# Reading the experts' weights in 8 KB pieces per partition, with the channels of their inputs reordered to match

## The chip, the core and the metric

The kernel runs on one core of a Trainium2 chip. A core has TensorE (PE in the profile; its weight loads are PEld), VectorE (DVE), ScalarE (ACT), GpSimd (POOL) and SyncE (SP), on-chip memory of 128 partitions (SBUF), accumulators for TensorE (PSUM) and 16 DMA engines between the chip's main memory (HBM) and SBUF. The metric is the device time of one execution, in microseconds (us). All data are float32. TensorE's fast format here is fp32r, so the kernel splits every operand into a rounded part and a remainder (hi and lo) and forms each product from three matmuls: hi x hi, lo x hi, hi x lo.

## The reference

Two layers of an encoder, 1024 tokens of 1024 channels. Each layer has a token-mixing half (attention and a convolution) and a routed feed-forward half, to which this change belongs:

```python
def expert_choice_ffn(h, w_router, w_gate, w_up, w_down):
    B, S, D = h.shape
    cap = CAPACITY_FACTOR * S // N_EXPERTS                 # 128 tokens
    logits = jnp.einsum('bsd,de->bse', h, w_router).astype(jnp.float32)
    aff = jax.nn.softmax(logits, axis=-1)
    gate, idx = lax.top_k(aff.transpose(0, 2, 1), cap)
    xe = jax.vmap(lambda hb, ib: hb[ib])(h, idx)
    hid = jax.nn.silu(jnp.einsum('becd,edf->becf', xe, w_gate)) * jnp.einsum('becd,edf->becf', xe, w_up)
    ye = jnp.einsum('becf,efd->becd', hid, w_down) * gate[..., None].astype(h.dtype)
    return jax.vmap(lambda ib, yb: jnp.zeros((S, D), yb.dtype).at[ib.reshape(-1)].add(yb.reshape(-1, D)))(idx, ye)
```

Each of the 16 experts takes its 128 best tokens (gather), computes silu(x Wg) * (x Wu), multiplies by Wd, scales, and adds the rows back to their tokens (scatter). Wg, Wu and Wd are 1024 x 1024 for each expert: 4 MB each in HBM, 12 MB an expert.

## The kernel before, in words

A layer runs in stages: token mixing, then the output projection tile by tile (8 tiles of 128 tokens, the loop `for t in range(TT)`), then the router's sort, then the 16 experts. The order of all instructions is written out by hand, and every engine runs its own in that order: an instruction that waits holds back all behind it on its engine.

**Output projection.** For each tile `mix_mm` multiplies, `mix_x` (L956, L957, DVE) adds the result to the residual in `xm`, `mix_norm` (L962, ACT, then two small POOL operations of `rstd`) makes the norm's factor, and `mix_h` makes the experts' input h2: L969 (DVE) scales `xm` by row and column, L970 adds a row vector, on POOL for tiles 5, 6 and 7 and on DVE for the others. `h2_store` writes the tile to HBM. The router's logits are computed from `xm`, not from h2, in `affine` (L1115 to L1119), and sorted on DVE.

**Experts.** The three matrices of all experts form a list of 192 chunks of 1 MB for each layer (`chunks`, four to a matrix). `load_w` (L1004, SP's queue) reads chunk i of a matrix, rows 256i to 256i+255, as two blocks of 128 rows: partition p gets row 256i + p and row 256i + 128 + p, two pieces of 4 KB that are no neighbours in HBM. A chunk lands in one of five raw buffers in `F`. `split_w` makes the rounded part on ACT (L118) and the remainder on DVE (L119) into one of seven working sets (`WS`, in the tiles R, flexX and flexC), and then issues the load of the chunk that gets the freed raw buffer. `product` multiplies 128 tokens by one matrix: for each of 4 chunks, 4 x 3 matmuls of 512 columns (L113 to L115), then the splits of later chunks, as far as `ahead()` allows: seven chunks at the layer's start, one less after every 8 chunks multiplied, and two from then on.

The order in one expert e is: product with Wu (up), `hid(...)`, `slots_1h` (L1285, 8 small DVE operations that prepare a later expert's gather), product of the next expert with its Wg (gate), in whose course `hid_t(e)` runs, `silu(...)`, product with Wd (down), `down_out` (L1358), which scales and scatters. `gather` (L1302, POOL's queue) fetches the next expert's 128 rows of h2, and `gather_t`/`trans` (L1314) transposes them on TensorE, so that channel 128k + p of a token lies in partition p of block k; this is the order in which the weight rows lie too.

`silu` (L1342, ACT) reads the gate product from PSUM and writes `sg`, two tiles of 512 hidden channels; `hid` (L1346, DVE) multiplies the up product from PSUM into `sg`; `hid_t` transposes `sg` (L504) and splits it.

```python
        hid(product(xT[e], {2: lambda: gather_t(e + 1, (0,)), 3: lambda: next_x(e + 1)}))
        s3 = e + 3 if e + 3 < NE else None
        if s3:
            slots_1h(s3)
        silu(product(xT[e + 1], {1: (lambda: slots(s3)) if s3 else (lambda: None), 2: lambda: hid_t(e)}))
        if e < NE - 2:
            down_out(e, product(hT2[e]))
```

Of the kernel before, what the change touches and what calls it, by code (L numbers as in the profile page):

```python
# [15 lines left out]
AF = mybir.ActivationFunctionType  # L16
ALU = mybir.AluOpType
AX = mybir.AxisListType
ADD, SUB, MUL = ALU.add, ALU.subtract, ALU.mult

T, D, KT, TT = 1024, 1024, 8, 8
# [4 lines left out]
NE, CAP = 16, 128  # L26
# [16 lines left out]
def trunk(ctx: ExitStack, tc: tile.TileContext, x, c, positions, norm1_g, w_ada, b_ada, w_in, q_latent_g, w_uq,  # L43
# [4 lines left out]
    v, a, g, pe, sp = nc.vector, nc.scalar, nc.gpsimd, nc.tensor, nc.sync  # L48
# [38 lines left out]
    def fw(o, *s):  # L87
        return _view(F, o, s)
# [12 lines left out]
    def ps_s():  # L101
        return psum.tile([128, 1024], F32, name="S")
# [32 lines left out]
    def rstd(dst, ss, n, cols=1):  # L135
        g.tensor_scalar(dst, ss, 1.0 / n, EPS, op0=MUL, op1=ADD)
        g.tensor_tensor(dst, dst, neghalf if cols == 1 else neghalf.to_broadcast([128, cols]), op=ALU.pow)
# [137 lines left out]
    TAPS = [[1, 0, 2, 0, 2, 2, 2, 1], [1, 1, 2, 1, 1, 1, 0, 1], [3, 6, 5], [4, 4], [0, 0, 7, 9, 7, 5, 5, 8], [5, 6], [5, 6], [0, 0, 8, 8, 6, 4, 6, 5], [[], 0, 1], [0], 1, 1, 0]  # L275

    def layer(l):
# [494 lines left out]
        for j, n in ((1, 0), (1, 1), (2, 0), (2, 1)):  # L772
            ps = ps_s()
# [88 lines left out]
        for u in range(U):  # L862
            hd, i = divmod(u, TT)
# [66 lines left out]
        g1, tg, a2, b2, g2 = (fw(o, 1024) for o in (0, 1024, 2048, 3072, VB + 1024))  # L930
        xt = lambda t: fw((8960, 4096)[t % 2] if t else 5120, 1024)
        xm = lambda t: fw((9984, 5120)[t % 2], 1024)
        h2 = lambda t: fw({TT - 2: 1024, TT - 1: 11008}.get(t, (8960, 4096)[t % 2]), 1024)
# [10 lines left out]
        MX, RS = {}, {}  # L944
# [14 lines left out]
        def mix_norm(t):  # L959
# [2 lines left out]
            a.activation(h2(t), xm(t), AF.Square, accum_out=ss)  # L962
            rstd(ss, ss, D)

        def h2_store(t):
            sp.dma_start(h2_d[l][128 * t:128 * t + 128], h2(t))

        def mix_h(t):
            v.scalar_tensor_tensor(h2(t), xm(t), RS[t], a2, op0=MUL, op1=MUL)  # L969
            (g if t == TT - 1 or t in TAPS[6] else v).tensor_tensor(h2(t), h2(t), b2, op=ADD)  # L970
            if t != TT - 2:
                h2_store(t)

# [9 lines left out]
        raw_of = lambda c: fw(11008 if c == 1 else RING[(c - 2) % 5 if c else 0], 4, 512)  # L983

        after = lambda c: 2 if c == 0 else None if c == 1 else c + 5

        WP = [w_gate[l, 0], w_up[l, 0]]
        for e in range(NE - 2):
            WP += [w_gate[l, e + 1], w_down[l, e], w_up[l, e + 1]]
        WP += [w_gate[l, NE - 1], w_up[l, NE - 1], w_down[l, NE - 2], w_down[l, NE - 1]]  # L990
        chunks = [(w, i) for w in WP for i in range(4)]
        NCH = len(chunks)


# [1 line left out]

        def load_w(c):
            if c is not None and c < NCH:
                w, i = chunks[c]
                w = w.rearrange("(k p) f -> p k f", p=128)  # L1000
                raw = raw_of(c).rearrange("p (k n) f -> p k (n f)", n=2)
                for ks in parts(c):
                    r = slice(ks.start // 2, ks.stop // 2)
                    sp.dma_start(raw[:, r], w[:, 2 * i + r.start:2 * i + r.stop])  # L1004

        sctr = [0]

        def split_w(sub=None):
            c = sctr[0]
            if c < NCH:  # L1010
                for ks in parts(c):
                    split(WS[c % NW][0][:, ks], WS[c % NW][1][:, ks], raw_of(c)[:, ks], sub)
                load_w(after(c))
                sctr[0] += 1
# [6 lines left out]
        def split_lo(c, q):  # L1021

            if q % 2 == 0:
                SP_[0] = ps_s()
            ps = SP_[0][:, 512 * (q % 2):512 * (q % 2) + 512]
            pe.matmul(ps, ident, raw_of(c)[:, q], start=True, stop=False)  # L1026
            pe.matmul(ps, neg, WS[c % NW][0][:, q], start=False, stop=True)  # L1027
            if q % 2:
                a.activation(WS[c % NW][1][:, q - 1:q + 1], SP_[0].rearrange("p (q c) -> p q c", q=2), AF.Copy)
            if q == 3:  # L1030
                load_w(after(c))
                sctr[0] += 1
# [88 lines left out]
        for t in range(TT):  # L1121
# [35 lines left out]
            if t == 0:  # L1157
                load_w(0)
                load_w(1)
                pc = ps_m()  # L1160
                for k in range(KT):
                    pe.matmul(pc[:, :NE], AB[l][:, 3, k:k + 1].to_broadcast([128, 128]), wr[:, k], start=(k == 0),
                              stop=(k == KT - 1))
                v.tensor_copy(cr, pc[:, :NE])
                v.scalar_tensor_tensor(a2, a2, 1.0, tg, op0=ADD, op1=MUL)
            else:
                mix_t(t - 1)
# [17 lines left out]
            if t == TT - 1:  # L1185
                load_w(3)
                h2_store(TT - 2)
                split_hi(2)
                if not TAPS[9][0]:
                    split_hi(3)  # L1190
# [11 lines left out]
            if t < TT - 1:  # L1202
                mix_h(t)
# [5 lines left out]
        logits(TT - 1, range(4), 4, 3)  # L1209
        split_lo(2, 2)  # L1210
        mix_h(TT - 1)
        affine(TT - 1)
        load_w(5)
# [108 lines left out]
        def product(lhs, hooks={}, upto=NCH):  # L1322
            ps = ps_s()
            for i in range(4):
                c = pctr[0]
                hl = WS[c % NW]
                for j in range(4):
                    kk, n = 2 * i + j // 2, j % 2
                    mm3(ps[:, 512 * n:512 * n + 512], lhs[0][:, kk], lhs[1][:, kk], hl[0][:, j], hl[1][:, j],
                        kk == 0, kk == KT - 1)  # L1330
                pctr[0] += 1
                while sctr[0] < min(upto, c + 1 + ahead()) and sctr[0] <= c + NW:
                    split_w()
                if i in hooks:
                    hooks[i]()
            return ps

        sg = fw(14688, 512), fw(16832, 512)

        def silu(ps):  # L1340
            for n in range(2):
                a.activation(sg[n], ps[:, 512 * n:512 * n + 512], AF.Silu)  # L1342

        def hid(ps):
            for n in range(2):
                v.tensor_tensor(sg[n], ps[:, 512 * n:512 * n + 512], sg[n], op=MUL)  # L1346

        def hid_t(e):
            hT2[e] = [rw(2048 * (e < NE - 1) + 1024 * i, KT, 128) for i in range(2)]
            for b in range(2):  # L1350
                p = to_heads(lambda k: sg[b][:, 128 * k:128 * k + 128])
                split(hT2[e][0][:, 4 * b:4 * b + 4], hT2[e][1][:, 4 * b:4 * b + 4], p.rearrange("p (k q) -> p k q", k=4))
# [22 lines left out]
        def second():  # L1375
            slots(1)
            gather(1)
            slots_1h(2)

        silu(product(xT[0], {0: second, 2: lambda: slots(2)}))  # L1380

        def next_x(e):
# [4 lines left out]
        for e in range(NE - 1):  # L1387
# [7 lines that stand above are left out]
        hid(product(xT[NE - 1]))  # L1395
        ps = product(hT2[NE - 2], {TAPS[11]: lambda: hid_t(NE - 1)})
        down_out(NE - 1, product(hT2[NE - 1], {TAPS[12]: lambda: down_out(NE - 2, ps)}))


    for l in range(L):  # L1400
        layer(l)
# [25 lines left out]
```

## Time and profile before

| | |
|---|---|
| median of 3 runs | 2317.97 us (2317.94 to 2320.8) |
| the profiled execution | 2317.1 us, span from first to last instruction 2315.3 us |
| PE busy | 2216.0 us (96%) |
| DVE busy | 1906.7 us (82%) |
| ACT busy | 1357.0 us (59%) |
| POOL busy | 430.0 us (19%) |
| bytes moved by DMA | 550.97 MB, mean 238 GB/s |
| loads of expert chunks | 128 + 128 + 126 of 1 MB, and 4 of 0.5 MB |
| granted TensorE clock, mean | 0.988 |

Busy time is the time in which an engine has an instruction running; waits in between are listed with what released them. The span of two layers shows the stages twice: from about 592 to 1160 us, and again from about 1730 to 2303 us, the experts run, and DMA and DVE are busiest; before that lie token mixing and the projection. The chain that ended last is followed back from the last instruction, at each step to what released it. An instruction in it delays the end by what it grows; one outside it does so only after its slack is used up.

### The profile page before, as it was taken

What the parts mean: (1) busy time and instruction counts of PE and PEld (TensorE: products, weight loads), DVE (VectorE), ACT (ScalarE), POOL (GpSimd) and SP (SyncE); (2) the same over time, 40 slices, a digit from 0 to 9 for tenths busy, and PEclk for the clock granted to TensorE, in tenths of its full rate; (3) what the DMA queues carried; (4) which work ended last, traced back from release to release, by engine and by line L of the source; (5) the groups of instructions that cost most, each with busy time, mean ns of one, the idle gap of its engine ahead of it and who ended that gap; (6) DMA issues with size and microseconds to landing.
All of it is one profiled execution on the core that took longest, in us unless ns stands there. A gap on an engine that the chain in (4) does not pass through costs nothing. (4 is left out here: it accounts for less than half of the span.)

```text
span 2315.3 us, 31226 instructions
## 1 busy us (share of the span) xinstructions
PE 2216.0 (96%) x11845; PEld 1798.5 (78%) x11845; DVE 1906.7 (82%) x2648; ACT 1357.0 (59%) x1770; POOL 430.0 (19%) x405
## 2 busy tenths in 40 slices
PE   6999999999999999999969999999999999999997
PEld 3678899886688787788847789888867878787786
DVE  3886888668889999998959868875688899999997
ACT  4324766623666677676741356665247667777675
POOL 1001212201021332322010021121011123231320
PEclk9999999999999999999979999999999999999999
DMA  8472000435899999999956300014369999999996
GB/s 276 160 250 90 18 4 19 142 124 199 291 334 352 378 381 380 372 387 376 356 143 213 135 12 16 1 45 161 124 228 331 340 363 382 379 369 390 377 379 239
DMA packets 179354, 550.97 MB, mean 238 GB/s; under 512 B 12820, under 2 KB 34470, under 8 KB 179204
## 3 DMA queue, kind: packets, MB, share of 16 engines
q1 hardware_dynamic: 169712, 515.35, 59.9%
q0 software_dynamic: 9216, 33.56, 5.6%
q8 instruction: 93, 1.52, 0.3%
q14 instruction: 57, 0.47, 0.1%
q10 hardware_dynamic: 276, 0.07, 0.0%
HBM read 515.35 MB, written 33.59 MB: 237 GB/s over the span
## 5 line engine op out<-in xcount | busy, mean ns | idle before, releaser
L119 DVE TENSOR_TENSOR R<-F,R 128x2048 fp32r<-128x2048 f32 (+1 forms) x294 | 636.5, 2185 | 74.7 <-ACT R L118 74.3
L118 ACT ACTIVATE R<-F 128x2048 fp32r<-128x2048 f32 (+1 forms) x294 | 533.3, 1832 | 66.0 <-DMA F<-in_w_up_dram 23.8
L115 PE MATMUL S<-R,flexX 128*128 128x512 f32 x1096 | 431.8, 394 | 10.0 <-DVE R L119 10.0
L113 PE MATMUL S<-R,flexX 128*128 128x512 f32 x1096 | 439.0, 401 | 0.0
L114 PE MATMUL S<-R,flexX 128*128 128x512 f32 x1096 | 427.6, 390 | 0.0
L304 DVE SCALAR_TENSOR_TENSOR F<-F,cw 128x1024 f32<-128x1024 f32 x240 | 307.6, 1282 | 5.3
L119 DVE TENSOR_TENSOR flexC<-F,flexC 128x2048 fp32r<-128x2048 f32 (+3 forms) x126 | 258.3, 2055 | 16.5 <-ACT flexC L118 16.4
L115 PEld LDWEIGHTS S<-R,flexX 128*128 128x128 f32 x1096 | 205.7, 188 | 64.1 <-DVE R L119 17.0
L118 ACT ACTIVATE flexC<-F 128x2048 fp32r<-128x2048 f32 (+3 forms) x126 | 216.9, 1728 | 49.6 <-DMA F<-in_w_in_dram 14.3
L114 PEld LDWEIGHTS S<-R,flexX 128*128 128x128 f32 x1096 | 206.1, 188 | 42.8 <-DVE flexX L119 0.3
L113 PEld LDWEIGHTS S<-R,flexX 128*128 128x128 f32 x1096 | 206.1, 188 | 39.7 <-ACT flexX L118 0.5
L118 ACT ACTIVATE flexX<-T 128x512 fp32r<-128x512 f32 x128 | 73.1, 597 | 238.3 <-PE T L1314 135.2
L115 PE MATMUL S<-R 128*128 128x512 f32 x480 | 189.5, 395 | 0.0
L113 PE MATMUL S<-flexC,flexX 128*128 128x512 f32 x440 | 176.3, 401 | 0.0
L115 PE MATMUL S<-flexC,flexX 128*128 128x512 f32 x440 | 173.3, 394 | 2.5 <-DVE flexC L119 2.5
L114 PE MATMUL S<-flexC,flexX 128*128 128x512 f32 x440 | 171.9, 391 | 2.4 <-DVE flexX L119 2.4
L1359 POOL DMA_INDIRECT x<-F,idx x16 | 99.9, 6245 | 389.9 <-DVE F L1358 364.5
L1359 POOL DMA_INDIRECT out_dram<-F,idx x16 | 99.1, 6193 | 390.1 <-DVE F L1358 364.7
L578 PE MATMUL m<-F 128*128 128x128 f32 x1024 | 125.2, 275 | 0.3
L578 PEld LDWEIGHTS m<-F 128*128 128x128 f32 x1024 | 119.4, 192 | 1.2 <-DVE R L510 1.2
L113 PE MATMUL S<-R 128*128 128x512 f32 x288 | 118.3, 411 | 0.0
L114 PE MATMUL S<-R 128*128 128x512 f32 x288 | 112.6, 391 | 0.0
(294 smaller groups left out, 4017.5 us busy)
## 6 DMA issues: line engine op xcount, KB each, us to landing
F<-in_w_gate_dram SPq DMA_DIRECT2D x128, 1024.0 KB
F<-in_w_up_dram SPq DMA_DIRECT2D x128, 1024.0 KB
F<-in_w_down_dram SPq DMA_DIRECT2D x126, 1024.0 KB
F<-in_w_ada_dram SPq DMA_DIRECT2D x42, 1024.0 KB
F<-in_x_dram SPq DMA_DIRECT2D x16, 512.0 KB
F<-in_w_in_dram SPq DMA_DIRECT2D x16, 512.0 KB
F<-in_w_out_dram SPq DMA_DIRECT2D x16, 512.0 KB
h<-F SPq DMA_DIRECT2D x16, 512.0 KB
```

The source lines that it names most:

```text
L113: pe.matmul(ps, lh, rh, start=first, stop=False)
L114: pe.matmul(ps, ll, rh, start=False, stop=False)
L115: pe.matmul(ps, lh, rl, start=False, stop=last)
L118: a.activation(hi, src, AF.Copy)
L119: (sub or v.tensor_sub)(lo, src, f32(hi))
L304: taps.append(lambda i=i: v.scalar_tensor_tensor(ACC[j], Y[j][:, i:i + T], w[:, i:i + 1], ACC[j], op0=MUL, op1=ADD))
L578: pe.matmul(po[:, :DV], PTS[u % 2][:, k], V[:, k], start=(k == 0), stop=(k == KT - 1))
L1359: g.indirect_dma_start(out=xm_d, out_offset=bass.IndirectOffsetOnAxis(ap=idx[:, e:e + 1], axis=0), in_=y, in_offset=None, compute_op=ADD)
```

## The change

Weight rows are dealt to the partitions differently. Of Wg and Wu, partition p holds rows 8p to 8p + 7, which are neighbours in HBM (32 KB), and a chunk reads two of these rows: one piece of 8 KB for each partition, 32 KB from the next partition's. Of Wd, partition p holds rows 4p to 4p + 3 of each half, and a chunk reads two of them: pieces of 8 KB, 16 KB apart. The bytes, the number of loads, the buffers and the order stay.

So block k of the experts' input must hold channels 8p + k, and block k of a half of the hidden values channels 4p + k of that half. The gather and the transposes stay as they are; the values are put in that order where they are written: L969, L970 (`mix_h`), L1342 (`silu`) and L1346 (`hid`) now write consecutive elements 128 elements (512 bytes) apart in SBUF, and L970 and L1346 read the operand that was written so with the same step. The same instructions run on every engine in the same sequence; only the access patterns of these four and of the loads differ.

```diff
+        by_row = lambda ap: ap.rearrange("q (p k) -> q p k", k=KT)
...
         def mix_h(t):
-            v.scalar_tensor_tensor(h2(t), xm(t), RS[t], a2, op0=MUL, op1=MUL)
-            (g if t == TT - 1 or t in TAPS[6] else v).tensor_tensor(h2(t), h2(t), b2, op=ADD)
+            hp = h2(t).rearrange("q (k p) -> q p k", k=KT)
+            v.scalar_tensor_tensor(hp, by_row(xm(t)), RS[t], by_row(a2), op0=MUL, op1=MUL)
+            (g if t == TT - 1 or t in TAPS[6] else v).tensor_tensor(hp, hp, by_row(b2), op=ADD)
...
-        WP = [w_gate[l, 0], w_up[l, 0]]
+        gate_w, up_w = ([w[l, e].rearrange("(p k) f -> p (k f)", k=8) for e in range(NE)] for w in (w_gate, w_up))
+        down_w = [w_down[l, e].rearrange("(n p k) f -> p n (k f)", n=2, k=4) for e in range(NE)]
+        WP = [gate_w[0], up_w[0]]
...
-        chunks = [(w, i) for w in WP for i in range(4)]
+        chunks = [w[:, i // 2, 2048 * (i % 2):2048 * (i % 2) + 2048] if len(w.shape) == 3 else w[:, 2048 * i:2048 * i + 2048]
+                  for w in WP for i in range(4)]
...
         def load_w(c):
             if c is not None and c < NCH:
-                w, i = chunks[c]
-                w = w.rearrange("(k p) f -> p k f", p=128)
-                raw = raw_of(c).rearrange("p (k n) f -> p k (n f)", n=2)
+                raw = raw_of(c).rearrange("p q f -> p (q f)")
                 for ks in parts(c):
-                    r = slice(ks.start // 2, ks.stop // 2)
-                    sp.dma_start(raw[:, r], w[:, 2 * i + r.start:2 * i + r.stop])
+                    r = slice(512 * ks.start, 512 * ks.stop)
+                    sp.dma_start(raw[:, r], chunks[c][:, r])
...
+        half = lambda ps, n: ps[:, 512 * n:512 * n + 512].rearrange("q (p k) -> q p k", k=4)
+        sgp = [s.rearrange("q (k p) -> q p k", k=4) for s in sg]
+
         def silu(ps):
             for n in range(2):
-                a.activation(sg[n], ps[:, 512 * n:512 * n + 512], AF.Silu)
+                a.activation(sgp[n], half(ps, n), AF.Silu)
 
         def hid(ps):
             for n in range(2):
-                v.tensor_tensor(sg[n], ps[:, 512 * n:512 * n + 512], sg[n], op=MUL)
+                v.tensor_tensor(sgp[n], half(ps, n), sgp[n], op=MUL)
```

## Rows read from the trace of the kernel before

**Rows 1.** Busy us by stretch; columns: window and length, PE, PEld, DVE, ACT, POOL (instructions), PEclk, DMA share, GB/s:

```profile
900.00:950.00 50.00, 48.77 (x239) 39.23 (x238) 45.51 (x53) 33.76 (x24) 14.61 (x4) 1.00 1.02 370
```

**Rows 2.** Chain that ended last: by engine, and one expert of it (start, us, what):

```profile
PE 20%; DVE 4%; ACT 1%; issue 1%; DMA 0%; POOLq 0%; DVEq 0%
...
2038.37 0.45 PE T L1314 x4
...
2039.33 1.92 ACT R L118
...
2044.16 0.36 DVE F L1346
2044.68 0.68 DVE F L1346
2045.36 1.30 DVE F L1285 x8
2046.66 2.21 DVE flexC L119
2048.92 0.50 PE S L115
```

**Rows 3.** Timeline of PE, first layer's experts (start, us, engine, what, [idle before <- releaser]):

```profile
662.40 0.66 PE L504 MATMUL T<-ident,F 128*128 128x128 f32 x4 [0.39 <-DVE idx L1293]
...
730.84 0.50 PE L115 MATMUL S<-R,flexX 128*128 128x512 f32 x1 [0.62 <-DVE R L119]
...
1055.35 0.50 PE L115 MATMUL S<-R,flexX 128*128 128x512 f32 x1 [0.62 <-DVE R L119]
```

**Rows 4.** Timeline of DVE and PE, the same place in the third expert:

```profile
692.54 2.29 DVE L119 TENSOR_TENSOR R<-F,R 128x2048 fp32r<-128x2048 f32 x1
...
694.90 0.40 PE L115 MATMUL S<-R,flexX 128*128 128x512 f32 x1
```

**Rows 5.** Groups of DVE by line and shape (count | busy us, mean ns of one | idle before):

```profile
L1346 DVE TENSOR_TENSOR F<-S,F 128x512 f32<-128x512 f32 x64 | 41.0, 683 | 0.0
...
L262 DVE TENSOR_TENSOR ab<-T,cols 128x4 f32<-128x4 f32 x16 | 2.6, 160 | 17.9 <-PE T L259 17.9
...
L1267 DVE TENSOR_TENSOR F<-F 128x128 bf16<-128x128 f32 x2 | 1.1, 528 | 0.1
...
L1236 DVE CAST F<-tok_b 128x128 bf16<-128x128 f32 x2 | 0.7, 332 | 0.0
...
L1271 DVE TENSOR_TENSOR F<-T,F 128x120 f32<-128x120 f32 x2 | 0.5, 273 | 0.0
...
L1271 DVE TENSOR_TENSOR F<-T,F 128x8 f32<-128x8 f32 x2 | 0.3, 172 | 0.0
```

**Rows 6.** Timeline of POOL and DVE at the projection's last two tiles, first layer:

```profile
564.48 2.35 POOL L970 TENSOR_TENSOR F<-F 128x1024 f32<-128x1024 f32 x1 [1.51 <-PE m L1109]
...
552.66 2.44 DVE L957 TENSOR_TENSOR F<-F 128x512 f32<-128x512 f32 x1
...
563.08 1.26 DVE L969 SCALAR_TENSOR_TENSOR F<-F,ss 128x1024 f32<-128x1024 f32 x1
...
565.42 1.84 DVE L1119 TENSOR_SCALAR F<-F,st 128x16 f32<-128x16 f32 x1
```

**Rows 7.** Timeline around one `silu`: ACT, DVE, PE:

```profile
917.43 1.09 ACT L1342 ACTIVATE F<-S 128x512 f32<-128x512 f32 x2 [0.32 <-PE S L115]
...
920.35 2.29 DVE L119 TENSOR_TENSOR flexC<-F,flexC 128x2048 fp32r<-128x2048 f32 x1 [0.92 <-ACT flexC L118]
...
923.18 0.39 PE L115 MATMUL S<-flexC,flexX 128*128 128x512 f32 x1
```

**Rows 8.** DMA: rates in 40 slices of 150 to 200 us; 900 to 1100 us; longest DMA wait, first layer's experts:

```profile
GB/s 403 411 396 283 2 29 238 408 408 398 216 174 403 403 393 283 34 202 401 411 400 257 10 180 392 411 410 288 0 149 383 391 177 0 0 0 0 0 0 7
...
DMA packets 19659, 75.53 MB, mean 378 GB/s; under 512 B 1245, under 2 KB 1245, under 8 KB 19648
...
ACT R L118 <- DMA F<-in_w_up_dram: 13.6, 19, 1.5
```

More of the change, by code (lines that the diff above doesn't have):

```diff
@@ L985, in layer @@
         after = lambda c: 2 if c == 0 else None if c == 1 else c + 5
-        WP = [w_gate[l, 0], w_up[l, 0]]
+        gate_w, up_w = ([w[l, e].rearrange("(p k) f -> p (k f)", k=8) for e in range(NE)] for w in (w_gate, w_up))
+        down_w = [w_down[l, e].rearrange("(n p k) f -> p n (k f)", n=2, k=4) for e in range(NE)]
+        WP = [gate_w[0], up_w[0]]
         for e in range(NE - 2):
-            WP += [w_gate[l, e + 1], w_down[l, e], w_up[l, e + 1]]
-        WP += [w_gate[l, NE - 1], w_up[l, NE - 1], w_down[l, NE - 2], w_down[l, NE - 1]]
-        chunks = [(w, i) for w in WP for i in range(4)]
+            WP += [gate_w[e + 1], down_w[e], up_w[e + 1]]
+        WP += [gate_w[NE - 1], up_w[NE - 1], down_w[NE - 2], down_w[NE - 1]]
+        chunks = [w[:, i // 2, 2048 * (i % 2):2048 * (i % 2) + 2048] if len(w.shape) == 3 else w[:, 2048 * i:2048 * i + 2048]
+                  for w in WP for i in range(4)]
         NCH = len(chunks)
```

## The prediction

> **What bounds the kernel now.** I read the windows first, then the chain that ended last, then the timelines of the waits it shows. In the experts' stage TensorE is busy for 48.8 of 50 us at full clock, DVE for 45.5, and the DMA share is 1.02 [rows 1]: three resources look full, and the share of busy time doesn't say which sets the pace. The chain does [rows 2]. It holds PE, DVE and ACT, and DMA rounds to 0%; the loads that this change speeds or slows aren't on it. One expert of it reads: transposes on PE (L1314), a split on ACT and DVE, then on DVE without a gap the two multiplications of `hid` (L1346), `slots_1h` (L1285), the next split (L119), and at its end the PE matmul that needs this split's remainder. So `hid` lies on the path, since the split queued behind it on DVE is what PE waits for.
>
> The stall is small, 0.62 us of idle PE, but it returns in each expert: ten times from 730.84 to 1055.35 us, 36.06 us apart [rows 3], and ten times again in the second layer. The second expert has a smaller one, also behind `hid` (0.39 us, at 662.40) [rows 3]. The third has none, but its split ends at 692.54 + 2.29 = 694.83 and PE uses it at 694.90 [rows 4]: a margin of 0.07 us. The first expert has more lead, and the last ones have no `slots_1h` in the way. That makes 12 experts a layer, 24 in all, in which any lengthening of `hid` goes straight into the time.
>
> **The loads.** 384 chunks of 1 MB come as before, in pieces of 8 KB in place of 4 KB. The rate in full stretches is 400 to 411 GB/s where w_ada is read in 2 KB pieces, and 378 on the average of 900 to 1100 us, with the gathers and scatters in it [rows 8]; pieces were not what held it down there. A faster load lands earlier, ACT's waits for DMA shrink (13.6 us in the first layer's experts for the largest group [rows 8]), and nothing on the chain moves, since the split before `hid` waits for PE's transposes and not for a load [rows 2]. I take 0 for the loads; what covers a slower one is the slack of the third rival below.
>
> **The price of a stride.** No row shows a float32 write with a step of 512 bytes. Consecutive elements cost VectorE (683 - 273) / (512 - 120) = 1.05 ns each, with 148 ns fixed [rows 5] (L1346, and the 120-element form of L1271, which is nearly contiguous). The nearest rows with a step:
> - L1271 on 8 elements 64 bytes apart, a tensor_tensor with one operand in PSUM, the other and the result strided, as in `hid`: 172 ns. Four contiguous elements from PSUM took 160 (L262), four more would be 4.2; the other 7.8 ns over 8 elements are 1.0 ns an element, one more cycle.
> - L1236, 128 elements written 10 bytes apart: 332 against 148 + 134 = 282 ns, 0.4 ns an element. This is the low end.
> - L1267, 128 elements read and written 10 bytes apart: 528 against 282, 1.9 ns an element. This is the high end.
>
> All three are dearer than contiguous. I take 1.0 ns, by L1271, the row nearest in form.
>
> [...]
>
> **The sum.**
> - `hid`: 2 x 512 elements x 1.0 ns = 1.0 us an expert, 24 experts on the path: **+24.0 us** (0.41 x 24 = 9.8 at the low end, 1.95 x 24 = 46.8 at the high one).
> - `mix_h`, L969: 1024 elements, +1.0 us (0.4 to 1.95). Tiles 0 to 5 have cover: PE multiplies throughout and DVE isn't what it waits for. At the last two tiles there is none: L969 of the last tile ends at 564.34, and the softmax of the last tile's logits queues right behind it on DVE, ahead of the sort [rows 6]. Two tiles in two layers: +4.0 us (1.6 to 7.8).
> - `mix_h`, L970 on POOL: it takes 2.35 us, and DVE's L957 and L1119, behind the last two tiles' adds, took 2.44 and 1.84 us and ended about when POOL did [rows 6], L1119 for 16 elements. DVE is held there until POOL is through, so what the add grows, the chain to the sort grows. No row shows POOL with a step. It is bounded by 0 and by a doubling, 2.35 us; I take the 1.0 us of DVE's row, lying between. Two adds in two layers: +4.0 us (0 to 9.4). For tile 5 the matmuls behind it cover the add.
> - `silu`, on ACT: 1.09 us for two, 0 to 2 us more. The split behind it is through at 920.35 + 2.29 = 922.64 on DVE, PE takes it at 923.18 [rows 7]: a margin of 0.54 us. ACT has no strided row at all; I take half of DVE's, 0.5 us, which the margin covers: 0. If it grows by 1.0, 0.46 x 24 = 11 us come on top.
> - `h2_store`, gather, transposes, matmuls, and the SP queue: the same instructions in the same places, 0.
>
> Together +32 us on the profiled execution's 2317.1 us: 2349.1. The median of the runs is 0.9 above that execution, which gives **2350 us**. The low ends together give +11.4, 2329; the high ends +64, 2383, and with a `silu` of that price (1.41 x 24 = 34) 2416.
>
> **The rivals.**
> 1. The strides cost nothing, or the loads' pieces change nothing either: 2318 us. For it: L1271's excess is 8 ns on a short instruction, where fixed costs are uncertain, and the two larger rows write 2-byte elements. Against it: three rows of three are dearer. Chance 0.23.
> 2. Faster. DMA sets the pace after all: a chunk's late landing delays ACT's split, DVE's behind it, and by the whole expert the split that PE waits for. With earlier landings the 10 stalls of 0.62 us in each layer go: 12.4 us, 2305 us. For it: the DMA share is 1.02 and ACT waited for loads [rows 1, 8]. Against it: the stalls are equal to hundredths over ten experts and both layers, and the split before `hid` waits for PE [rows 2, 3]. It decides only if the strides cost less than the 0.6 us of a stall. Chance 0.10.
> 3. The loads get slower: the 128 pieces of a load, neighbours before, now lie 32 or 16 KB apart. With `hid` grown an expert takes 37.1 us, for which 378 x 36.06 / 37.06 = 368 GB/s are needed; below that, loads set the pace, and at 340 GB/s an expert takes 40.1 us: about 24 x 4 = 97 us over the time before, 2415. The pieces of w_ada, 24 KB apart, reached 400 GB/s and more [rows 8], which speaks against it. Chance 0.04. [...]
>
> **How the numbers follow.** The forecast with its bounds, 2329 to 2383, has 0.59, the joint high end above 2385 about 0.04. A run of this kernel tells about 0.2%, 4.6 us, from no change. Slower by more takes the forecast, its high end and rival 3: 0.67. Same takes rival 1: 0.23. Faster takes rival 2: 0.10. For 8 in 10 the range goes from 2313, which takes in rival 1, to 2385; it leaves out most of rival 2, rival 3 and the joint high end, less than 0.2. The likeliest case's own range is 2329 to 2383.
>
> **What will show it.** Right: the row of `hid` (683 ns) grows to about 1.2 us and L969 (1.26) to 2.3; PE's stall behind `hid` grows from 0.62 to about 1.6 us in each expert, and experts stand 37.1 us apart; L1119 of the last tile and POOL's add grow together; ACT's waits for DMA shrink or stay, without effect. Wrong: `hid` stays at 683 ns (rival 1 or 2), the stall goes (rival 2), PE or ACT waits for loads at lengths of microseconds (rival 3), or `hid` grows and the experts' distance doesn't, which would mean that DVE had slack that I don't see.

## The result, and the profile after

The change is slower: 2368.68 us in the median of 4 runs (2364.89 to 2376.73), against 2319.12 (2317.94 to 2320.8) for the kernel before on the same chip. The ratio is 1.0218, 95% interval 1.0206 to 1.0230. That is +49.6 us where the forecast had +32: inside the range of 2313 to 2385, the direction right, the sum too small. The profiled execution took 2364.89 us, its span is 2363.1, that is 47.8 more than the span before.

In the changed file the lines have moved: `mix_h` is L973 and L974 (L969, L970 before), `silu` L1351 (L1342), `hid` L1355 (L1346), the softmax's last step L1125 (L1119), `slots_1h` L1291, `trans` L1320. First the groups of instructions by line and shape (count | busy us, mean ns of one | idle before) of the changed kernel, for the four that write with a step; behind them the same of the kernel before for `mix_h` on DVE and `silu`:

```profile
L1355 DVE TENSOR_TENSOR F<-S,F 128x512 f32<-128x512 f32 x64 | 67.4, 1100 | 0.0
L1351 ACT ACTIVATE F<-S 128x512 f32<-128x512 f32 x64 | 66.6, 1151 | 12.9 <-PE S L115 12.9
L973 DVE SCALAR_TENSOR_TENSOR F<-F,ss 128x1024 f32<-128x1024 f32 x16 | 32.7, 2044 | 15.7 <-POOL ss L137 15.6
...
L974 DVE TENSOR_TENSOR F<-F 128x1024 f32<-128x1024 f32 x10 | 19.8, 1983 | 0.3
L974 POOL TENSOR_TENSOR F<-F 128x1024 f32<-128x1024 f32 x6 | 17.5, 2918 | 13.2 <-PE m L1115 8.9 <-DVE F L973 4.4
```

```profile
L1342 ACT ACTIVATE F<-S 128x512 f32<-128x512 f32 x64 | 34.8, 596 | 12.7 <-PE S L115 12.7
L969 DVE SCALAR_TENSOR_TENSOR F<-F,ss 128x1024 f32<-128x1024 f32 x16 | 20.5, 1280 | 15.7 <-POOL ss L137 15.4
L970 DVE TENSOR_TENSOR F<-F 128x1024 f32<-128x1024 f32 x10 | 12.2, 1225 | 0.3
```

All four grew. `hid` stood at 683 ns [rows 5]: 417 ns more for 512 elements, 0.81 ns each. L973 was 1280 ns, so 0.75 ns an element more; L974 on DVE was 1225 (+0.74), on POOL 2364 (+0.54). `silu` was 596: 555 ns more, 1.08 ns an element, the dearest of all, and it is on ACT, for which there had been no row.

Next the timeline of PE in the first layer's experts (start, us, engine, what, [idle before <- releaser]), to be held against the same places in [rows 3, 4]:

```profile
667.29 0.66 PE L504 MATMUL T<-ident,F 128*128 128x128 f32 x4 [1.17 <-DVE idx L1299]
...
703.06 0.66 PE L504 MATMUL T<-ident,F 128*128 128x128 f32 x4 [0.36 <-DVE idx L1299]
...
774.53 0.50 PE L115 MATMUL S<-R,flexX 128*128 128x512 f32 x1 [1.45 <-DVE R L119]
786.95 0.51 PE L115 MATMUL S<-R,flexX 128*128 128x512 f32 x1 [0.26 <-DVE R L119]
811.91 0.50 PE L115 MATMUL S<-R,flexX 128*128 128x512 f32 x1 [1.45 <-DVE R L119]
```

The stall behind `hid` is 1.45 us where it was 0.62, the second expert's 1.17 where it was 0.39, and the third expert, which had a margin of 0.07, now has one of 0.36. Behind `hid` of the fourteenth and fifteenth expert there was none before; now there are 0.47 and 0.44 us. Behind twelve of a layer's `silu`s there is a second stall, of 0.22 to 0.28 us, that wasn't there before. Around `silu` the timeline shows why:

```profile
894.55 2.10 ACT L1351 ACTIVATE F<-S 128x512 f32<-128x512 f32 x2 [0.31 <-PE S L115]
...
896.43 1.94 ACT L118 ACTIVATE R<-F 128x2048 fp32r<-128x2048 f32 x1
...
898.40 2.29 DVE L119 TENSOR_TENSOR R<-F,R 128x2048 fp32r<-128x2048 f32 x1 [1.81 <-ACT R L118]
...
900.75 0.50 PE L115 MATMUL S<-R,flexX 128*128 128x512 f32 x1 [0.27 <-DVE R L119]
```

Two `silu` take 2.10 us where they took 1.09 [rows 7]. The split queued behind them on ACT starts a microsecond later, DVE's remainder too, and PE waits for it: the margin of 0.54 is used up. From expert to expert it is 811.91 - 774.53 = 37.38 us, where it was 36.06.

The first expert has a longer stall as well. These are its rows before the change, with it, and in a run described below that has all of the change except the step in `silu`:

```profile
617.77 0.50 PE L114 MATMUL S<-flexC,flexX 128*128 128x512 f32 x1 [1.22 <-DVE flexX L119]
621.88 0.50 PE L114 MATMUL S<-flexC,flexX 128*128 128x512 f32 x1 [2.08 <-DVE flexX L119]
621.62 0.50 PE L114 MATMUL S<-flexC,flexX 128*128 128x512 f32 x1 [1.21 <-DVE flexX L119]
```

This stall stands ahead of the first `hid`, and with `hid` alone made plain it stays at 2.12 us. So its growth of 0.86 us is `silu`'s.

The tail of the output projection, first layer: first one row of PE from the trace of before, then rows of PE and DVE with the change (POOL's adds stand at 538.15, 554.59 and 568.18 there and take 2.96, 2.94 and 2.86 us).

```profile
541.75 0.27 PE L1062 MATMUL T<-ident,F 128*32 128x128 f32 x1
```

```profile
543.04 0.27 PE L1068 MATMUL T<-ident,F 128*32 128x128 f32 x1 [1.67 <-DVE F L1125]
...
555.01 3.07 DVE L957 TENSOR_TENSOR F<-F 128x512 f32<-128x512 f32 x1
...
569.23 2.23 DVE L1125 TENSOR_SCALAR F<-F,st 128x16 f32<-128x16 f32 x1
...
571.61 0.27 PE L1068 MATMUL T<-ident,F 128*32 128x128 f32 x1 [2.33 <-DVE F L1125]
```

L957 and L1125 end 0.55 and 0.42 us after POOL's adds, as they did before (0.55 and 0.43), when they took 2.44 and 1.84 us [rows 6]. They are longer by 0.63 and 0.39 us; the adds grew by 0.55 and 0.51. But PE also stalls for 1.67 us at 543.04, behind the add of tile 5, which I had taken as covered. At the same place before (L1062) it has no idle time.

Now the loads. In the window of busy time that [rows 1] show, with the same columns, the rate is lower:

```profile
900.00:950.00 50.00, 48.03 (x223) 38.42 (x222) 46.81 (x40) 35.67 (x24) 13.63 (x3) 1.00 0.98 365
```

ACT's waits for DMA in the first layer's experts (total us, times, longest) are fewer and longer, with the same total; there were 19 of up to 1.5 us [rows 8]:

```profile
ACT R L118 <- DMA F<-in_w_up_dram: 13.7, 10, 2.5
```

365 GB/s are no sign of slow loads: the slower pace asks for 370 x 36.06 / 37.38 = 357.

The starts of the same instructions split the 47.8 us by stage. The first gather's transposes start at 593.52 (590.29 before): 3.2 us from the first layer's `mix_h`. The next layer's last L356 starts at 1391.0 (1367.2): another 20.6 for the first layer's experts. The second layer's transposes start at 1757.76 (1727.95): 6.0 more for its `mix_h`; the rest, 18.0, is its experts. Experts 38.6 us, `mix_h` 9.2. Of the first layer's experts, 1.6 us are a fall of TensorE's clock (last section).

### The profile page after: what moved, and what is told of

It reads as the page before. It is cut to its first block, busy times and chain, and to the rows that moved or that the text cites. A ratio compares the mean times of both kernels' runs of the same rounds, so it can differ in the third digit from the quotient of the medians.

```text
span 2363.1 us, 31228 instructions
## 1 busy us (share of the span) xinstructions
PE 2227.4 (94%) x11845; PEld 1800.0 (76%) x11845; DVE 1955.6 (83%) x2648; ACT 1380.8 (58%) x1770; POOL 445.0 (19%) x405
## 5 line engine op out<-in xcount | busy, mean ns | idle before, releaser
L115 PE MATMUL S<-R,flexX 128*128 128x512 f32 x1096 | 434.1, 396 | 28.5 <-DVE R L119 28.5
L115 PEld LDWEIGHTS S<-R,flexX 128*128 128x128 f32 x1096 | 205.8, 188 | 89.9 <-DVE R L119 44.1
L115 PE MATMUL S<-R 128*128 128x512 f32 x480 | 189.7, 395 | 0.0
L1368 POOL DMA_INDIRECT x<-F,idx x16 | 105.5, 6592 | 409.2 <-DVE F L1367 383.8
L115 PE MATMUL S<-flexC,flexX 128*128 128x512 f32 x440 | 174.6, 397 | 8.2 <-DVE flexC L119 8.2
```

The lines of the kernel that those rows point to most:

```text
L115: pe.matmul(ps, lh, rl, start=False, stop=last)
L1368: g.indirect_dma_start(out=xm_d, out_offset=bass.IndirectOffsetOnAxis(ap=idx[:, e:e + 1], axis=0), in_=y, in_offset=None, compute_op=ADD)
```

## The experiments

**Loads or strides?** My theory was that the loads cost nothing and the strides everything; the rivals, that the new loads bring time back or cost some. Two kernels do one part each.

The loads alone: `load_w` and `chunks` as in the change, `mix_h`, `silu` and `hid` as before.

> The weights are read in the new order and in 8 KB pieces, but h2 and the hidden values are written in the old order, so that the products mix wrong channels; the amount of work is the same. My theory (the strided writes are the whole cost, loads have slack): 2318 us within 5, experts 36.06 us apart, stall behind hid 0.62 us. Rival (the loads are slower, their late landings are part of the 50 us): over 2325 us, ACT waits for loads for microseconds. Rival (the loads were a bound): under 2313 us.

Measured: 2317.46 us (11 runs) against 2318.78 (15 runs of before), ratio 0.9997, 0.9988 to 1.0006. Its window shows PE, DVE and the DMA share as [rows 1] do, and in its timeline of PE the stalls behind `hid` are those of before, 0.60 to 0.64 us in the first layer, 36.05 us from the one shown to the next:

```profile
900.00:950.00 50.00, 48.79 (x240) 39.28 (x239) 45.50 (x53) 34.54 (x26) 13.56 (x4) 1.00 1.01 378
```

```profile
765.91 0.51 PE L115 MATMUL S<-R,flexX 128*128 128x512 f32 x1 [0.63 <-DVE R L119]
```

The strides alone: the old loads, the four instructions as in the change.

> The kernel before, its loads in the old order and in 4 KB pieces, with the four strided writes of the change, so that the products mix wrong channels. My theory: the same as the change, 2365 to 2369 us, experts 37.4 us apart. Rival (loads take a part): clearly less, by as much as the loads alone add.

Measured: 2369.4 us (2365.66 to 2375.11), ratio 1.0217, 1.0198 to 1.0237; `hid` 1099 ns, `silu` 1150, `mix_h` 2045. The strides are the whole of it, and pieces of 8 KB that lie 32 or 16 KB apart in HBM are worth as much here as pieces of 4 KB, to within 0.12%.

**Which of the strides?** Three kernels take the step out of one of the places each, and leave the change otherwise as it is.

```diff
-                v.tensor_tensor(sgp[n], half(ps, n), sgp[n], op=MUL)
+                v.tensor_tensor(sg[n], ps[:, 512 * n:512 * n + 512], sg[n], op=MUL)
```

> The change with hid alone put back to contiguous (its product then pairs wrong hidden channels). hid measured 683 to 1100 ns, so 0.83 us for two, on the path of 12 experts in each of two layers: 20 us less than the change, about 2347. If DVE had slack elsewhere: less than 10 us.

Measured: 2344.67 us (2341.47 to 2346.35), 24.0 less than the change's median. The first stall is back at 0.62, the second stays:

```profile
778.40 0.51 PE L115 MATMUL S<-R,flexX 128*128 128x512 f32 x1 [0.62 <-DVE R L119]
790.82 0.50 PE L115 MATMUL S<-R,flexX 128*128 128x512 f32 x1 [0.24 <-DVE R L119]
```

Now `silu`:

```diff
-                a.activation(sgp[n], half(ps, n), AF.Silu)
+                a.activation(sg[n], ps[:, 512 * n:512 * n + 512], AF.Silu)
```

> The change with silu alone put back to contiguous (hid then pairs wrong hidden channels). silu measured 597 to 1151 ns, 1.1 us for two, of which the margin of 0.54 us covers half: 0.5 to 0.6 us in 12 to 14 experts a layer, 12 to 16 us less than the change, about 2353. If silu was covered, as predicted: no change.

Measured: 2352.08 us (2349.11 to 2354.91), 16.6 less. The second stall is gone, the first stays, and the experts stand 36.92 us apart:

```profile
773.74 0.50 PE L115 MATMUL S<-R,flexX 128*128 128x512 f32 x1 [1.44 <-DVE R L119]
...
810.66 0.50 PE L115 MATMUL S<-R,flexX 128*128 128x512 f32 x1 [1.44 <-DVE R L119]
```

So `silu` costs 37.38 - 36.92 = 0.46 us in an expert with the second stall. That is what the pair of instructions grew, 2.10 - 1.09 = 1.01 us, less the margin of 0.54. PE's idle time shows only 0.26 of it; a part of the rest is that the matmul after a stall takes 0.50 us and the others 0.39 or 0.40.

And `mix_h` (L973, L974 as L969, L970 before):

> The change with mix_h alone put back to contiguous (the gathered channels then don't match the weights' rows). Measured: L969 grew by 0.77 us, POOL's add by 0.56 us, both counted at the last two tiles of two layers: 5.3 us less than the change; with what the earlier runs leave over of the 50 us (24 for hid, 17 for silu) up to 9 us less, 2360 to 2364 us. Rival (the earlier tiles count too, about 1.5 us each): 20 us less or more.

Measured: 2355.0 us (2354.36 to 2355.73), 13.7 less by medians and 9.2 by the profiled spans (2363.1 - 2353.9), 2360 to 2364 expected: a miss, in the direction of a dearer `mix_h`. The stall that was left out is tile 5's: (0.77 + 0.56) us for tiles 6 and 7 in two layers are 5.3, and 1.67 twice for tile 5 another 3.3: 8.7. The total agrees with the 9.2 better than its parts do: `mix_h` cost 3.2 us in the first layer and 6.0 in the second. The rows explain 4.3 in each; I did not follow the rest through the sort.

By medians the three parts are 24.0 + 16.6 + 13.7 = 54.3, by spans 19.1 + 15.8 + 9.2 = 44.1; the whole is 49.6 and 47.8. The change's four runs spread over 12 us, and single spans hold falls of the clock at different places (it is 0.83 from 850 to 860 us in the change, 0.80 from 625 to 630 with `hid` plain), so neither sum is sharp. Distances inside a trace are sharper. In the second layer's experts the granted clock is 1.00 in all the traces compared here. From the start of the first `silu` to the start of the last matmul on L115 it is, before and with the change:

```profile
1745.26 1.09 ACT L1342 ACTIVATE F<-S 128x512 f32<-128x512 f32 x2
2302.59 0.40 PE L115 MATMUL S<-R,flexX 128*128 128x512 f32 x1
```

```profile
1774.96 2.06 ACT L1351 ACTIVATE F<-S 128x512 f32<-128x512 f32 x2
2350.36 0.40 PE L115 MATMUL S<-R,flexX 128*128 128x512 f32 x1
```

That is 557.33 us and 575.40 us: 18.07 us more. With `hid` plain the same distance is 2331.49 - 1767.32 = 564.17, and with `silu` plain 2334.48 - 1766.03 = 568.45. So `hid` costs 11.23 us a layer and `silu` 6.95, and the two add up to 18.18, within 0.11 of the whole. For two layers that is 22.5 us for `hid` and 13.9 for `silu`. The order of the three parts is the same by all three measures.

**What is it about the stride?** `silu` and `hid` of successive experts write with another step.

```diff
+            k = 1 << turn[0] % 10
...
-                a.activation(sgp[n], half(ps, n), AF.Silu)
+                a.activation(sg[n].rearrange("q (k p) -> q p k", k=k), half(ps, n, k), AF.Silu)
```

> The change, but from one expert to the next silu and hid write with another step: 4 bytes (contiguous, two of ten experts), 8, 16, 32, 64, 128, 256, 512 and 1024 bytes. The same elements are written, to other places, so the down product sums over hidden channels that don't belong to its rows, and the output is not the layer's. Theory 1, that every write to a new line of 16 bytes costs the same: hid takes 0.68 us with steps of 4 bytes, 0.8 to 0.9 with 8, and 1.10 with every step from 16 to 1024 bytes; silu 0.60, 0.8 to 0.9, and 1.15. The time is then about 2360 us. Theory 2, that the price comes from the step of 512 bytes (or powers of two above it) falling on the same part of the memory: hid and silu stay at 0.68 and 0.60 us up to some step between 64 and 256 bytes, and only from there on cost 1.10 and 1.15; the time is about 2335 to 2345 us.

The timelines of DVE and then of ACT (two instructions in each row). Down the rows of `hid` (here L1361) the step is 1024, 16, 8 and 4 bytes; down those of `silu` (here L1355) 16 and 8 bytes (with 4 bytes it takes 1.09 us, as in [rows 7]):

```profile
627.96 2.06 DVE L1361 TENSOR_TENSOR F<-S,F 128x512 f32<-128x512 f32 x2
...
851.24 2.09 DVE L1361 TENSOR_TENSOR F<-S,F 128x512 f32<-128x512 f32 x2
888.09 1.28 DVE L1361 TENSOR_TENSOR F<-S,F 128x512 f32<-128x512 f32 x2
924.13 1.28 DVE L1361 TENSOR_TENSOR F<-S,F 128x512 f32<-128x512 f32 x2
```

```profile
825.74 2.06 ACT L1355 ACTIVATE F<-S 128x512 f32<-128x512 f32 x2 [0.28 <-PE S L115]
863.13 1.16 ACT L1355 ACTIVATE F<-S 128x512 f32<-128x512 f32 x2 [0.31 <-PE S L115]
```

The price is a cliff: with a step of 8 bytes nothing on DVE (1.28 us for two instructions, as with 4) and 0.07 us for two on ACT (1.16 against 1.09), all of it from 16 bytes on (2.09 and 2.06), and no more at 1024 (2.06 and 2.05). Between them on DVE, 64 bytes took 2.09 us, 256 and 512 took 2.13 and 2.11, but 32 took 2.37 and 128 took 2.26. These two excesses come again when the same steps come round once more in the first layer (2.34 and 2.23) and are not explained. Theory 2 falls. Of theory 1 one number was wrong: 8 bytes, for which it had 0.8 to 0.9 us an instruction, are as good as 4. Its lines of 16 bytes are not shown: the runs give the time at each step, not its cause. The time was 2366.35 us in one run, 2360 expected; it is too near the change's own spread to say more.

**Do reads pay as writes do?** The values can be put in the same places by walking the output in the order of memory and taking the step in the reads: 16 bytes in PSUM for `silu` and `hid`, 32 bytes in SBUF for `mix_h`.

```diff
-        by_row = lambda ap: ap.rearrange("q (p k) -> q p k", k=KT)
+        by_row = lambda ap: ap.rearrange("q (p k) -> q k p", k=KT)
...
-            hp = h2(t).rearrange("q (k p) -> q p k", k=KT)
+            hp = h2(t).rearrange("q (k p) -> q k p", k=KT)
...
-        half = lambda ps, n: ps[:, 512 * n:512 * n + 512].rearrange("q (p k) -> q p k", k=4)
-        sgp = [s.rearrange("q (k p) -> q p k", k=4) for s in sg]
+        half = lambda ps, n: ps[:, 512 * n:512 * n + 512].rearrange("q (p k) -> q k p", k=4)
+        sgp = [s.rearrange("q (k p) -> q k p", k=4) for s in sg]
```

> The change, with the same elements at the same places, but each of the four instructions walks its output in the order of memory: writes are contiguous, and the reads take the step instead (16 bytes from PSUM in silu and hid, 32 bytes from SBUF in mix_h). Theory 1, that only writes pay for a new line: hid 0.68 us, silu 0.60, L973 1.28, L974 1.23 on DVE and 2.36 on POOL; 2319 us, within 0.2% of before. Theory 2, that reads pay as writes do: hid 1.10, silu 1.15, L973 2.0; 2369 us as the change. Between them: reads from SBUF pay and reads from PSUM don't, so that mix_h alone costs its 9 to 14 us: 2328 to 2333.

Measured: 2331.7 us (2328.8 to 2334.48), ratio 1.0053, 1.0039 to 1.0066: the case between. Its groups by line and shape follow; the stalls behind `hid` in the first layer are back at 0.60 to 0.64 us.

```profile
L1355 DVE TENSOR_TENSOR F<-S,F 128x512 f32<-128x512 f32 x64 | 41.0, 682 | 0.0
L973 DVE SCALAR_TENSOR_TENSOR F<-F,ss 128x1024 f32<-128x1024 f32 x16 | 35.9, 2242 | 15.7 <-POOL ss L137 15.4
L1351 ACT ACTIVATE F<-S 128x512 f32<-128x512 f32 x64 | 34.8, 596 | 12.8 <-PE S L115 12.7
...
L974 DVE TENSOR_TENSOR F<-F 128x1024 f32<-128x1024 f32 x10 | 21.2, 2119 | 0.3
L974 POOL TENSOR_TENSOR F<-F 128x1024 f32<-128x1024 f32 x6 | 18.2, 3035 | 14.6 <-PE m L1115 9.1 <-PE S L1033 5.5
```

From PSUM the step is free on DVE and on ACT: 682 and 596 ns, as before the change (683 and 596). From SBUF it takes DVE 7 to 10% more time than a strided write: 2242 ns for L973, which now reads two operands with a step and writes none (2044 in the change, where it only writes with one), 2119 for L974 on DVE with one operand strided (1983 in the change, where it reads one and writes with a step). The prices of read and write don't add up. The swap of two loops in four instructions gives back 37.0 of the 49.6 us.

**TensorE does the reordering.** The loads of the change, all writes contiguous, and the transposes of the gather and of `hid_t` read their input with a step of 32 or 16 bytes.

```diff
-            trans(xT[e], fw(13664, 1024), bs)
+            trans(xT[e], fw(13664, 1024).rearrange("q (p k) -> q k p", k=KT), bs)
...
-                p = to_heads(lambda k: sg[b][:, 128 * k:128 * k + 128])
+                p = to_heads(lambda k: sg[b].rearrange("q (p k) -> q k p", k=4)[:, k])
```

> The reordering moved from the four writes to the transposes, which read every 8th or every 4th element on TensorE; mix_h, silu and hid are contiguous again, the loads are the change's; the result is the reference's. If a strided read costs TensorE nothing: 2318 us within 5, as with the loads alone. If each of the 16 transposes of an expert costs what a strided write costs on DVE, 0.8 ns for each of 128 columns, 0.1 us: 1.7 us an expert, on the path, 50 us more, 2370 us.

Measured: 2322.82 us (9 runs, 2319.49 to 2328.43), ratio 1.0022, 1.0012 to 1.0032. The price shows in PEld, the weight loads. In the first layer's experts (600 to 1160 us), the transposes of the gather and of `hid_t`, before and in this run:

```profile
L1314 PEld LDWEIGHTS T<-ident,F 128*128 128x128 f32 x120 | 14.9, 140 | 3.9
L504 PEld LDWEIGHTS T<-ident,F 128*128 128x128 f32 x128 | 14.9, 140 | 2.7 <-DVE idx L1293 0.6
```

```profile
L1319 PEld LDWEIGHTS T<-ident,F 128*128 128x128 f32 x120 | 18.0, 190 | 2.4
L504 PEld LDWEIGHTS T<-ident,F 128*128 128x128 f32 x128 | 18.1, 208 | 1.8 <-DVE idx L1298 0.5
```

A weight load takes 50 ns more with a step of 32 bytes and 68 more with one of 16. For the 8 transposes of each kind in an expert that is 0.94 us, and most of it is hidden: the matmuls of the gather's transposes take 274 ns instead of 272 (means of both layers), those of `hid_t` go from 273 to 283, and the experts stand 1054.54 - 1018.40 = 36.14 us apart instead of 36.06. This kernel computes the layer with 8 KB pieces and costs 4 us, against 49.6.

**The stall itself.** The chain showed `slots_1h` between `hid` and the split [rows 2]. Moving it into the gate product, behind its first chunk, takes 1.30 us out of that place without touching a stride; `slots`, which needs it, goes behind the last chunk.

```diff
+            hooks = {2: lambda: hid_t(e)}
             if s3:
-                slots_1h(s3)
-            silu(product(xT[e + 1], {1: (lambda: slots(s3)) if s3 else (lambda: None), 2: lambda: hid_t(e)}))
+                hooks.update({0: lambda: slots_1h(s3), 3: lambda: slots(s3)})
+            silu(product(xT[e + 1], hooks))
```

In the kernel before:

> The kernel before with slots_1h (1.3 us on DVE) moved from behind hid to behind the next product's first split, and its matmuls two chunks later. If the queue on DVE, hid, slots_1h, split, is what PE waits for: the stall of 0.62 us (0.78 us of lost pace) behind hid goes in 12 experts of two layers, up to 19 us less than before, about 2300 us. If PE waits for something else there (the loads, ACT): 2318 us.

In the change:

> The change with the same move of slots_1h. If the growth of hid costs time only because it stands in that queue: the stall falls from 1.45 us to under 0.2 us, 30 us less than the change or more, about 2335 us; what silu and mix_h add stays. If hid's growth costs through DVE's total load: less than 10 us less.

Measured: the kernel before falls to 2302.17 us (2300.67 to 2304.28), ratio 0.9930, 0.9916 to 0.9943. That is 16.6 us less than without the move, and faster than both kernels. PE's stall is gone: in the windows it is busy for all of the 50 us where it had 48.77 [rows 1].

```profile
900.00:950.00 50.00, 50.00 (x244) 40.80 (x243) 47.94 (x51) 37.65 (x28) 7.66 (x3) 1.00 1.03 394
```

The change falls to 2340.65 us (2337.31 to 2345.33), 28 less than without the move. 30 or more was expected, and a stall under 0.2 us; 0.43 to 0.47 us is left in twelve experts of the first layer, and they come 814.32 - 778.22 = 36.10 us apart. The rows of DVE and PE show that it is `hid`'s:

```profile
773.85 2.12 DVE L1355 TENSOR_TENSOR F<-S,F 128x512 f32<-128x512 f32 x2
775.87 2.29 DVE L119 TENSOR_TENSOR R<-F,R 128x2048 fp32r<-128x2048 f32 x1
...
778.22 0.50 PE L115 MATMUL S<-R,flexX 128*128 128x512 f32 x1 [0.45 <-DVE R L119]
...
814.32 0.50 PE L115 MATMUL S<-R,flexX 128*128 128x512 f32 x1 [0.47 <-DVE R L119]
```

DVE goes from `hid` to the split without a gap, the split ends at 778.16, and PE starts at 778.22. `silu`'s second stall is gone until the last two experts.

**Do the loads matter at that faster pace?** At 394 GB/s, where the window had 370 [rows 1], the loads may have less slack, so the loads alone once more, with this move:

> The new loads with all writes contiguous as before, and slots_1h and slots moved as in the run that had the old loads. The products multiply a channel by another channel's weights, so the output is not the layer's. Theory 1: the loads cost and bring nothing at this pace either: 2302 us, within 0.2% of the run with the old loads. Rival: at 0.7 us an expert less, loads begin to set the pace, and pieces of 8 KB land sooner: 2 us or more below 2300. Other rival: pieces 32 KB apart are slower once there is no slack: 2306 or more.

Measured: 2301.4 us (2299.38 to 2304.62), ratio 0.9929, 0.9916 to 0.9943. The same as with the old loads. And the strided reads with the move:

> As the run before it, and slots_1h and slots moved to the first and the last chunk of the gate product. Theory 1 (only writes pay): 2302 us, as the kernel before with this move, faster than both kernels by 16 us or more. Theory 2 (reads pay as writes): 2341 us, as the change with this move. Between them (SBUF alone): 2311 to 2316.

Measured: 2316.06 us (11 runs, 2313.02 to 2318.74), ratio 0.9985, 0.9976 to 0.9994: the case between again, at its upper end; `mix_h` costs 13.9 us against the kernel before with this move. That kernel, at 2302.17 us, stays the fastest of those that compute the layer.

## Why the prediction was right in direction and too small

- **What bounds the kernel.** Right. The stall behind `hid` is on the path in each expert, and all that `hid` grew went into it (0.62 to 1.45 us for 0.83 us of growth). Taking `slots_1h` out of it gave 16.6 us. The experts stand 37.38 us apart, where I had said 37.1. That this is near is in part luck: `hid` alone makes it 36.92, less than I said, and `silu` adds 0.46.
- **The loads at 0.** Right, at both paces: 0.9997 (0.9988 to 1.0006), and 2301.4 against 2302.17 us. Rivals 2 and 3 are out.
- **`hid`, +24.0.** Measured 22.5 us by distances (24.0 by medians, 19.1 by spans). It is near because two errors cancel. The price was too high: 0.81 ns an element, 0.83 us an expert, where I took 1.0; that this is "one more cycle" was my reading, which no run shows. The count was too low: the stall grew in 14 experts a layer, not in 12, since the fourteenth and the fifteenth, which I had left out, now stall too.
- **`silu` at 0.** This is the step that failed. "I take half of DVE's, 0.5 us, which the margin covers": the pair grew by 1.01 us, nearly twice the margin of 0.54. It cost 13.9 us by distances (16.6 by medians, 15.8 by spans, which hold 1.6 of a fallen clock). The prediction's own alternative, 0.46 x 24 = 11, is right for the 12 experts a layer with a second stall; it lacks the first expert, 0.86 us in each layer. I had no row of ACT with a step and chose the value that the margin hid; a margin of half a microsecond should have put the odds the other way.
- **`mix_h`, +8.0.** The two prices were too high (0.75 and 0.54 ns an element where I took 1.0), and "for tile 5 the matmuls behind it cover the add" was wrong: PE stalls there for 1.67 us in each layer, where the trace of before lists no idle time at that place. The two errors nearly cancel: 8.7 by the rows, 9.2 by spans. That is luck, too.
- **The sums.** The high end is 1 us too high as written: 2317.1 + 64.0 + 0.9 = 2382, not 2383. Nothing hangs on it.
- **The spread.** Not foreseen: 11.8 us over 4 runs, where the kernel before has 2.9.

## What to carry to other kernels

When a layout change puts a permutation into an instruction that is already there, price it by its step: float32 values written to SBUF 512 bytes apart cost 0.54 ns more an element on POOL, 0.74 to 0.81 on DVE and 1.08 on ACT here. In `hid` and `silu` the price was there from 16 bytes on (2.09 us for two instructions on DVE and 2.06 on ACT, where contiguous ones took 1.28 and 1.09), and 8 bytes cost next to nothing (1.28 and 1.16). Put the step into a read from PSUM or into TensorE's transposes, which cost nothing and 0.08 us an expert here, and leave writes to SBUF on DVE, ACT and POOL, and reads of it on DVE and POOL (2242 and 2119 ns for 1280 and 1225, and 3035 for 2364), contiguous. And before costing a growth at nothing because a margin covers it, take the dearest price that the rows allow: the margin was 0.54 us, the growth 1.01.

## What the runs showed of the hardware that I had not expected

- A step of 16 bytes in the read from PSUM is free on DVE and ACT (682 and 596 ns). On DVE a step in SBUF costs nearly the same for reads as for writes, and both together cost it once (1983 ns with both, 2044 with a strided write alone and 2119 with a strided read alone, where 1225 and 1280 are contiguous).
- ACT pays more for a strided write (1.08 ns more an element with 512 bytes) than DVE (0.81), though it is no slower on contiguous ones (596 and 683 ns for 512).
- A weight load of TensorE that reads SBUF with a step takes 190 ns (32 bytes) or 208 (16 bytes) instead of 140, and most of it is hidden behind matmuls: 36.14 us an expert instead of 36.06.
- After one stall of 1.45 us the granted clock fell to 0.50. These are windows of the change around the stall that ends at 849.33 (columns as in [rows 1]; the third from the end is the clock):

```profile
847.00:849.00 2.00, 0.88 (x11) 0.45 (x10) 2.00 (x2) 0.63 (x1) 0.00 (x0) 1.00 1.02 338
849.00:851.00 2.00, 1.67 (x6) 1.40 (x7) 2.00 (x2) 0.00 (x0) 0.00 (x0) 0.84 1.01 420
851.00:853.00 2.00, 2.00 (x6) 1.41 (x6) 1.93 (x6) 0.00 (x0) 0.00 (x0) 0.50 1.02 385
```

  That expert took 888.31 - 849.33 = 38.98 us, 1.6 more than its neighbours. The run with the strides alone shows the same fall after its stall that ends at 853.05 (0.78 from 855 to 860 us, and 38.94 us to the next stall), and the run with `hid` plain shows one behind the first expert's stall of 2.12 us (0.80 from 625 to 630 us, 0.86 from 630 to 635). The same stall in the change's other experts had no such effect, and the kernel before, with stalls of 0.62, shows no fall inside its experts. The slowest of the change's four runs had a mean clock of 0.936, the other three 0.986 or 0.987; that falls like this one make its spread is argued, not shown.
